# Where the operands of single-pass matmuls begin in SBUF: 128 and 448 past a multiple of 512 bytes, or at the multiple

## The chip, the cores and the metric

The kernel runs on one core of one Trainium2 chip. The metric is the device time of one execution in microseconds, the median over several runs; lower is better.

## What is computed

Two transformer blocks run one after the other on one sequence of 256 tokens and 1024 features, all in float32 with weights from HBM. The first block (two layers) has a SwiGLU on either side of a mixer; the mixer of layer 0 joins a spatial gate with a three-way sparse attention, that of layer 1 a causal pooling with a diagonal state-space scan. The second block (two layers) has a mixer of three branches (retention, a gated recurrence, a sliding-window attention with sinks), then a SwiGLU in layer 0 and a top-2 mixture of eight experts in layer 1. Cut to what matters here:

```python
def swiglu(h, w_gate, w_up, w_down):
    return (jax.nn.silu(h @ w_gate) * (h @ w_up)) @ w_down

# first block, each layer:
x = x + 0.5 * swiglu(rmsnorm(x, g0), ...)
x = x + mixer(rmsnorm(x, g1))
x = x + 0.5 * swiglu(rmsnorm(x, g2), ...)
# second block, each layer:
proj = h @ w_in[layer]                       # 1024 x 11776
merged = sig(ga) * y_a + sig(gb) * y_b + sig(gc) * y_c
h = layer_norm(ALPHA * h + merged @ w_o[layer])
h = layer_norm(ALPHA * h + (swiglu_2(h) if layer == 0 else moe_swiglu(h)))
```

Nearly all of the arithmetic is products of the 256 tokens with weight matrices that are each read once.

## The kernel before, in words

**Weights as a stream.** The host packs all weights in the order of their use into chunks of 128 partitions x 2048 float32 (1 MB): 332 "dense" chunks, then 336 for the experts. `Stream.load` (L142) brings a chunk into one of four `raw` buffers (eleven in the expert stage) on SP's queue. `Stream.split_to` cuts it into pieces of 1024 columns: ScalarE rounds a piece to the reduced type float32r (`wh`, L159), VectorE subtracts to get the rest (`wl`, L160). `Stream.get` hands out slices of 512 columns or less.

**Single-pass matmuls.** A float32 product is made of three matmuls of float32r operands, each of one pass, summed in PSUM: high x high, and twice high x low. `mm3w` (L252 on) holds the weights stationary and streams the activations: 128 stationary columns, 256 moving ones (`xh`, `xl`, and `hh`, `hl` within a SwiGLU). `mm3x` holds the activations stationary and streams 512 weight columns: some projections of the mixers (`proj_x_steps`), the last output projection, and all expert matmuls (`gate_up`, `down`: stationary `gxh`, `gxl`, `mhh`, `mhl`). All go through `mm` (L250). There are 18,709 such matmuls in the program. Small products that need full precision run in plain float32 and are not the matter here.

**Where tiles lie.** Every tile is a byte range that is the same in all partitions. Pools follow each other in SBUF from low to high addresses: `one` (residual `x`, `xh`, `xl`), `raw`, a small pool `two` of 320 bytes (a vector table and a constant column), `hi` and `lo` (four buffers each of `wh`, `wl`, 4096 bytes apart), `wk`, and then pools that open and close stage by stage. `gap(pool, n, name)` takes n unused bytes of a pool, so that what follows begins n bytes later. The large operand tiles have sizes that are multiples of 512 bytes, so where a slice begins modulo 512 is settled by where its tile begins. Modulo 512, before the change:

| stage | moving operand | stationary operand |
|---|---|---|
| SwiGLUs, mixers, weights stationary | xh, hh, ah, gh, ch, yh, oh: 128 | wh, wl: 448 |
| mixers, weights moving | wh, wl: 448 | xh, oh: 128 |
| experts, gate, up, down | wh, wl: 448 | gxh, mhh: 256 |
| experts, gather of tokens | P: 256 | xh: 128 |
| experts, return of rows | yhl: 128 | PT: 384 |

**Order.** The order of instructions on each engine is that of the recorded program; tiles wait for their last readers. The lines that matter are L186 to L198 (`Net.__init__`), L224 on (`setup`), the `gap` calls in `even`, `odd`, `moe`, `run`, `run_last`, and the argument `free` of `ffn_core`, which is a gap ahead of `hh`.

Of the kernel before, what the change touches and what calls it, by code (L numbers as in the profile page):

```python
# [9 lines left out]
F32 = mybir.dt.float32  # L10
# [25 lines left out]
N_RAW, N_EXTRA = 4, 7  # L36
# [72 lines left out]
VOFF, NVEC = {}, {}  # L109
# [8 lines left out]
class Stream:  # L118
# [3 lines left out]
    def __init__(self, tc, dram, pools, split_ahead=4, extra=None):  # L122

        self.tc, self.nc, self.dram = tc, tc.nc, dram
        self.raw_p, self.hi_p, self.lo_p = pools
        self.specs = []
        self.pos = 0
        self.raw, self.hi, self.lo = {}, {}, {}
        self.loaded = self.split = 0
        self.extra = extra  # L130
        self.ahead, self.split_ahead = N_RAW - 1 + (N_EXTRA if extra else 0), split_ahead
        self.total = dram.shape[0]
# [45 lines left out]
def gap(pool, n, name):  # L178

    pool.tile([128, n // 4], F32, name="gap_" + name)


class Net:
    def __init__(self, ctx, tc, a, consts):  # L186
        self.tc, self.nc, self.a = tc, tc.nc, a
        self.ctx = ctx
        self.cn = consts
        pool = lambda n, b, **k: ctx.enter_context(tc.tile_pool(name=n, bufs=b, **k))  # L190
        self.one = pool("one", 1)
        self.raw_p = pool("raw", N_RAW)
        self.two = pool("two", 1)
        self.hi_p, self.lo_p = pool("hi", 4), pool("lo", 4)
        self.wk = pool("wk", 2)
        self.pa = pool("pa", 4, space=PSUM)
        self.pb = pool("pb", 4, space=PSUM)
        self.ws = Stream(tc, a["dense"], (self.raw_p, self.hi_p, self.lo_p))  # L198
# [25 lines left out]
    def setup(self):  # L224
        nc = self.nc
        self.ctx1 = self.ctx.enter_context(ExitStack())
        one1 = self.ctx1.enter_context(self.tc.tile_pool(name="one1", bufs=1, reuse_waits="tile"))
        self.vecs = {v: p.tile([128, NVEC[v]], F32, name=v) for v, p in (("vecs1", one1), ("vecs2", self.two))}
        nc.scalar.dma_start(self.vecs["vecs1"], self.a["vecs1"])
        self.x = self.one.tile([128, KD, S], F32, name="x")  # L230
        self.ws.load_to(0, [lambda s=slice(2 * d, 2 * d + 2): nc.sync.dma_start(self.x[:, s], self.a["xt"][:, s])
                            for d in range(4)])
        self.ws.split_to(1)
        self.ws.load_to(1)
        self.ident = self.consts(self.one, "all")["ident"]
        nc.gpsimd.dma_start(self.vecs["vecs2"], self.a["vecs2"])
        self.ones = self.one.tile([128, 128], F32, name="ones")
        nc.vector.memset(self.ones, 1.0)
        self.mhalf = self.two.tile([128, 16], F32, name="mhalf")
        nc.vector.memset(self.mhalf, -0.5)  # L240
        self.xh = self.one.tile([128, KD, S], F32R, name="xh")
        self.xl = self.one.tile([128, KD, S], F32R, name="xl")
# [219 lines left out]
    def even(self):  # L462
# [5 lines left out]
        with tc.tile_pool(name="ev", bufs=1, reuse_waits="tile") as P:  # L468
# [8 lines left out]
            for i in range(2):  # L477
# [6 lines left out]
                v = kv.rearrange("p g (n r) -> p r g n", r=8)  # L484
# [44 lines left out]
                nc.scalar.activation(vt[:, t], o[t], AF.Copy, scale=rc[:, t:t + 1])  # L529


            gap(P, 96, "a")
            ah = P.tile([128, 4, S], F32R, name="ah")
            al = P.tile([128, 4, S], F32R, name="al")
            tr = nc.tensor.transpose
# [100 lines left out]
            rv = self.rstd_cols(ms[:, 1], 16, 1.0 / 64, 1e-5)  # L636
            nc.vector.tensor_mul(vg, vg, rv[:, :, None].to_broadcast([128, 16, 64]))
            gap(P, 320, "g")
            gh = P.tile([128, 4, S], F32R, name="gh")
            gl = P.tile([128, 4, S], F32R, name="gl")  # L640
# [142 lines left out]
    def odd(self):  # L783
# [1 line left out]
        factors = self.rms_in(self.vec("norm", 32, 8))  # L785
        w, idx = "od_w_in", (0,)
        with tc.tile_pool(name="od", bufs=1, reuse_waits="tile") as P:
            gap(P, 448, "od")
            pm = self.consts(P, "odd")["pool"]
            pw = self.load(P, "pw", [128, 4, 128], self.a["pw"])  # L790
            u = P.tile([128, 4, S], F32, name="s5u")
# [63 lines left out]
            def pooling():  # L855

                for o in self.proj_x_steps([(w, idx, 0, 512)], 512, self.xh, self.xl):
                    yield
                zc = P.tile([128, 2, 512], F32, name="zc")
                for t in range(2):  # L860
                    nc.scalar.activation(zc[:, t], o[t], AF.Copy, scale=rc[:, t:t + 1])
                for g in range(4):
                    b = self.pbank((128, 512), "a")
                    s = slice(128 * g, 128 * g + 128)
                    self.mm(b[:, :256], zc[:, 0, s], pm[:, 384 * g:384 * g + 256], True, False)
                    self.mm(b[:, 128:256], zc[:, 1, s], pm[:, 384 * g + 256:384 * g + 384], False, True)
                    pl = W.tile([128, S], F32, name="pl", tag="t256", bufs=4)
                    nc.scalar.activation(pl, b[:, :S], AF.Copy)
                    b = self.pbank((128, 512), "a")
                    self.mm(b[:, :S], pw[:, g], pl, True, True)  # L870
                    yc = W.tile([128, S], F32, name="yc", tag="t256", bufs=4)
                    nc.scalar.activation(yc, b[:, :S], AF.Copy, scale=self.vec("pscale", g))
                    self.split(ch[:, g], cl[:, g], yc)
                    if g % 2:
                        yield
                for d in range(KD // 2):
                    for n, b in enumerate(self.proj_t_steps([("od_w_out", idx, d * 256, 256)], ch, cl, 4)):
                        if n % 2:
                            yield
                    self.add_out(d, b)  # L880

            steps = pooling()
            bu, a, z, py = {}, {}, {}, {}
# [495 lines left out]
        self.ln_finish(self.vec("lnmix", 0, 8), self.vec("lnmix", 8, 8))  # L1379

    def ffn2(self):
        self.ffn_core("ffn_w_gate_2", "ffn_w_up_2", "ffn_w_down_2", (0,), (0,), None, self.residual2, free=128)
        self.ln_finish(self.vec("lnffn", 0, 8), self.vec("lnffn", 8, 8))

    def ln_stats(self, x):
# [35 lines left out]
    def moe(self):  # L1421
        nc, tc, W = self.nc, self.tc, self.wk
        V = nc.vector
        Z = self.mo
        x = self.hx
        C = self.consts(Z, "moe")
        gap(Z, 256, "mo")
        cr = Z.tile([128, 2, 128], F32R, name="cr")
        V.tensor_copy(cr[:, 0], C["before"])
        V.tensor_copy(cr[:, 1], self.ones)  # L1430
# [81 lines left out]
        def one_hot(ep):  # L1512
            P = Z.tile([128, 2, 2, 128], F32R, name="P")
            for e in range(2):
                for t in range(2):
                    V.tensor_scalar(P[:, t, e], C["iota"][:, :128], pos[:, t, 2 * ep + e:2 * ep + e + 1], None,
                                    op0=OP.is_equal)
            return P
# [72 lines left out]
        P = one_hot(0)  # L1591
        G = gather(P)
        for e in range(NE):
            y = None
            pend = None
            for fb in range(8):
# [9 lines left out]
                if fb == 3 and e % 2 and e + 1 < NE:  # L1606
                    P = one_hot(e // 2 + 1)
# [122 lines left out]
    def run(self):  # L1730
        tc = self.tc
        self.setup()
        with tc.tile_pool(name="evw", bufs=1, reuse_waits="tile") as P:
            steps = self.even_loads(P)
            self.ffn1(0, 0, steps, free=352)
            for _ in steps:
                pass
            self.even()
        with tc.tile_pool(name="s5p", bufs=1, reuse_waits="tile") as P2:
            with tc.tile_pool(name="s5q", bufs=1, reuse_waits="tile") as P:  # L1740
                steps = self.s5_params(P, P2)
                self.ffn1(0, 1, steps, free=128)
                self.ffn1(1, 0, steps, free=128)
                for _ in steps:
                    pass
            self.odd()
        self.ffn1(1, 1, after=self.between)
        self.ctx1.close()
        with tc.tile_pool(name="l2", bufs=1, reuse_waits="tile") as Q:
            self.l2 = Q  # L1750
            gap(Q, 128, "l2")
            self.layer0()
        self.ffn2()
        self.run_last()

    def run_last(self):

        tc = self.tc
        with ExitStack() as self.ctx2:
            self.mo = self.ctx2.enter_context(tc.tile_pool(name="hxp", bufs=1))  # L1760
            with tc.tile_pool(name="l2b", bufs=1, reuse_waits="tile") as Q:
                self.l2 = Q
                gap(Q, 128, "l2")
                self.layer1()
            self.mo = self.ctx2.enter_context(tc.tile_pool(name="mo", bufs=1, reuse_waits="tile"))
            self.moe()
            self.overflow()
            self.out()
# [86 lines left out]
```

## Time and profile before

| | us |
|---|---|
| median of 3 runs | 3130.25 |
| the three runs | 3129.6, 3130.25, 3144.65 |
| the profiled execution's own time | 3141.89 |
| its span in the trace | 3140.1 |

The profile comes from one execution that took 3141.89 us, 11.6 us more than the median; its 1.8 us beside the span lie ahead of the first and behind the last instruction. The columns of the page: PE is TensorE's matmuls, PEld its weight loads, which overlap the matmuls, DVE VectorE, ACT ScalarE, POOL GpSimd. A matmul's record begins where it begins to stream and ends when its last result is written, so records of successive matmuls overlap: the time that a matmul costs is the step from its start to the start of the next, not its own duration. A row of a timeline gives start, duration, engine, line and operands; a row of windows gives a stretch and, per engine, busy time and the count of records that touch the stretch.

### The profile page before, as it was taken

To read this page: it belongs to the slowest core of one execution; us is meant where nothing else is said; L and a number is where in the kernel's file an instruction comes from. 1 tells how busy PE (TensorE), PEld (TensorE's weight loads), DVE (VectorE), ACT (ScalarE), POOL (GpSimd) and SP (SyncE) were. 2 spreads that over 40 slices of the span, in tenths; PEclk is the share of its full clock that TensorE was granted. 3 is DMA by queue.
4 is the path that set the end of the run, shared out by engine and by line. 5 is a ranking of instruction groups with operands and counts; after the bars stand their busy time and mean duration, and the time that the engine had idled before them with its cause. 6 is when DMAs were issued, how large, how long until landed. Compare 5 with 4: busy or idle time off the path is not lost. (4 is left out here: it accounts for less than half of the span.)

```text
span 3140.1 us, 51830 instructions
## 1 busy us (share of the span) xinstructions
PE 3046.8 (97%) x20841; PEld 2748.4 (88%) x20841; DVE 2341.3 (75%) x3444; ACT 1855.7 (59%) x2527; POOL 187.2 (6%) x159
## 2 busy tenths in 40 slices
PE   8999999999999999999999999989999999999998
PEld 8997999996899899899998898977787878878876
DVE  6667777868766675566556765568999899999888
ACT  5456555542543655554546654447777777777775
POOL 1000000002102000112010000010000000000000
PEclk9999999999999999999999999989999999999999
DMA  7542555551454333454553334658998998998994
GB/s 251 209 163 95 178 190 185 184 204 54 175 188 177 127 130 135 174 191 154 195 188 121 121 124 178 250 191 336 347 367 330 348 359 338 360 353 332 358 359 152
DMA packets 97414, 696.37 MB, mean 222 GB/s; under 512 B 10880, under 2 KB 11232, under 8 KB 13456
## 3 DMA queue, kind: packets, MB, share of 16 engines
q1 hardware_dynamic: 95184, 685.81, 59.3%
q0 software_dynamic: 752, 3.85, 0.4%
q8 instruction: 165, 2.70, 0.3%
q10 hardware_dynamic: 1232, 3.34, 0.3%
q14 instruction: 81, 0.66, 0.1%
HBM read 691.92 MB, written 1.05 MB: 221 GB/s over the span
## 5 line engine op out<-in xcount | busy, mean ns | idle before, releaser
L160 DVE TENSOR_TENSOR wl<-raw,wh 128x1024 fp32r<-128x1024 f32 x1299 | 1587.0, 1238 | 499.9 <-ACT wh L159 492.0
L159 ACT ACTIVATE wh<-raw 128x1024 fp32r<-128x1024 f32 x1299 | 1363.1, 1060 | 800.2 <-PE pa L250 639.8
L250 PE MATMUL pa<-xh,wh 128*128 128x256 f32 x3072 | 867.5, 283 | 13.2 <-ACT wh L159 9.8
L250 PE MATMUL pa<-xl,wh 128*128 128x256 f32 x3072 | 865.4, 282 | 4.1 <-DVE xl L348 3.9
L250 PE MATMUL pa<-xh,wl 128*128 128x256 f32 x3072 | 864.2, 281 | 0.5 <-DVE wl L160 0.5
L250 PEld LDWEIGHTS pa<-xh,wh 128*128 128x128 f32 x3072 | 585.5, 191 | 17.3 <-ACT wh L159 9.8
L250 PEld LDWEIGHTS pa<-xl,wh 128*128 128x128 f32 x3072 | 584.2, 190 | 6.6 <-DVE xl L348 5.3
L250 PEld LDWEIGHTS pa<-xh,wl 128*128 128x128 f32 x3072 | 587.3, 191 | 1.1 <-DVE wl L160 0.8
L250 PE MATMUL pa<-wl,gxh 128*128 128x512 f32 x896 | 354.6, 396 | 1.3 <-DVE wl L160 1.3
L250 PE MATMUL pa<-wh,gxl 128*128 128x512 f32 x896 | 354.2, 395 | 0.0
L250 PE MATMUL pa<-wh,gxh 128*128 128x512 f32 x896 | 323.2, 395 | 0.0
L250 PE MATMUL pa<-hh,wl 128*128 128x256 f32 x880 | 246.0, 280 | 0.0
L250 PE MATMUL pa<-hl,wh 128*128 128x256 f32 x880 | 245.9, 279 | 0.0
L250 PE MATMUL pa<-hh,wh 128*128 128x256 f32 x880 | 245.8, 279 | 0.0
L250 PEld LDWEIGHTS pa<-wl,gxh 128*128 128x128 f32 x896 | 168.4, 188 | 43.9 <-DVE wl L160 3.4
L250 PEld LDWEIGHTS pa<-wh,gxh 128*128 128x128 f32 x896 | 168.4, 188 | 40.7
L250 PEld LDWEIGHTS pa<-wh,gxl 128*128 128x128 f32 x896 | 168.3, 188 | 40.5
L250 PE MATMUL pb<-wl,mhh 128*128 128x512 f32 x448 | 179.2, 400 | 0.0
L250 PE MATMUL pb<-wh,mhl 128*128 128x512 f32 x448 | 177.8, 397 | 0.0
L250 PEld LDWEIGHTS pa<-hh,wl 128*128 128x128 f32 x880 | 167.3, 190 | 0.1
L250 PEld LDWEIGHTS pa<-hh,wh 128*128 128x128 f32 x880 | 165.5, 188 | 0.0
L250 PEld LDWEIGHTS pa<-hl,wh 128*128 128x128 f32 x880 | 165.2, 188 | 0.0
(506 smaller groups left out, 4041.3 us busy)
## 6 DMA issues: line engine op xcount, KB each, us to landing
raw<-in_moe SPq DMA_DIRECT2D x336, 1024.0 KB, 5.5
raw<-in_dense SPq DMA_DIRECT2D x315, 1024.0 KB, 4.8
c_lay<-in_c_lay POOLq DMA_DIRECT2D x2, 1152.0 KB, 6.9
x<-in_xt SPq DMA_DIRECT2D x4, 256.0 KB, 5.8
raw<-in_dense SPq DMA_DIRECT2D x4, 256.0 KB, 6.7
w<-in_cw ACTq DMA_DIRECT2D x1, 1024.0 KB, 8.1
out_dram<-hx SPq DMA_DIRECT2D x2, 512.0 KB, 2.6
c_odd<-in_c_odd POOLq DMA_DIRECT2D x1, 768.0 KB, 4.5
```

The costliest lines, as they stand in the source:

```text
L159: self.nc.scalar.activation(h, src, AF.Copy)
L160: self.nc.vector.tensor_sub(l, src, h)
L250: self.nc.tensor.matmul(out, l, r, start=start, stop=stop, skip_group_check=True)
```

## The change

No operation, shape, buffer count or order changes. Pool `two` goes; its two tiles and 64 unused bytes stand at the front of `one`, which moves `x`, `xh`, `xl` and `raw`, `hi`, `lo` to multiples of 512. The gaps are set anew so that the operand tiles of each stage begin there too:

```diff
         self.one = pool("one", 1)
-        self.raw_p = pool("raw", N_RAW)
-        self.two = pool("two", 1)
-        self.hi_p, self.lo_p = pool("hi", 4), pool("lo", 4)
+        self.vecs = {"vecs2": self.one.tile([128, NVEC["vecs2"]], F32, name="vecs2")}
+        self.mhalf = self.one.tile([128, 16], F32, name="mhalf")
+        gap(self.one, 64, "x")
+        self.raw_p, self.hi_p, self.lo_p = pool("raw", N_RAW), pool("hi", 4), pool("lo", 4)
...
-            gap(P, 96, "a")
+            gap(P, 416, "a")
...
-            gap(P, 448, "od")
+            gap(P, 256, "od")
...
-        self.ffn_core("ffn_w_gate_2", "ffn_w_up_2", "ffn_w_down_2", (0,), (0,), None, self.residual2, free=128)
+        self.ffn_core("ffn_w_gate_2", "ffn_w_up_2", "ffn_w_down_2", (0,), (0,), None, self.residual2, free=448)
...
-        gap(Z, 256, "mo")
+        gap(Z, 448, "mo")
...
-            self.ffn1(0, 0, steps, free=352)
+            self.ffn1(0, 0, steps, free=160)
...
-                self.ffn1(0, 1, steps, free=128)
-                self.ffn1(1, 0, steps, free=128)
+                self.ffn1(0, 1, steps, free=448)
+                self.ffn1(1, 0, steps, free=448)
...
-        self.ffn1(1, 1, after=self.between)
+        self.ffn1(1, 1, after=self.between, free=320)
...
-            gap(Q, 128, "l2")
+            gap(Q, 448, "l2")
...
-                gap(Q, 128, "l2")
+                gap(Q, 64, "l2")
```

Behind it every moving and every stationary operand of the table above begins at 0 modulo 512, with three exceptions: in the second block's last mixer `oh`, `ol` begin at 128 (against 0 for the weights), `PT` begins at 128, and the tiny operand `selr` of the router at 448. The distance from the moving to the stationary operand modulo 512, which was 320 or 192, is 0 in nearly all matmuls. Tiles of other instructions shift along.

One wait moves on POOL's queue, since the tile that a load writes over has another neighbour now. Here is the place ahead of the second block's first mixer, where the constants of the mixer (`c_lay`) and a vector table are loaded. Before:

```order
63 L945 TENSOR_TENSOR acc<-acc 128x256 [waits Pool_49]
64 L207 DMA c_lay<-in_c_lay 128x2304 [waits DMAHW5_49,DMASW2_49,PE_49]
65 L207 DMA vecs_11692<-in_vecs 128x50 [waits DMASW3_49]
66 L1725 MEMSET KA_11694 128x512
67 L1725 MEMSET KB_11695 128x768
```

And in the change:

```order
63 L944 TENSOR_TENSOR acc<-acc 128x256 [waits Pool_49]
64 L207 DMA c_lay<-in_c_lay 128x2304 [waits DMASW3_49,DMAHW5_49,DMASW2_49,PE_49]
65 L207 DMA vecs_11691<-in_vecs 128x50
66 L1724 MEMSET KA_11693 128x512
67 L1724 MEMSET KB_11694 128x768
```

The first of the two loads waits for what the second had waited for: an earlier load on POOL's own queue.

## Rows read from the trace of the kernel before

**Rows 1.** Page, parts 1 and 5: shares and costliest groups.

```profile
PE 3046.8 (97%) x20841; PEld 2748.4 (88%) x20841; DVE 2341.3 (75%) x3444; ACT 1855.7 (59%) x2527; POOL 187.2 (6%) x159
...
L250 PE MATMUL pa<-xh,wh 128*128 128x256 f32 x3072 | 867.5, 283 | 13.2 <-ACT wh L159 9.8
...
L250 PE MATMUL pa<-wl,gxh 128*128 128x512 f32 x896 | 354.6, 396 | 1.3 <-DVE wl L160 1.3
...
L250 PE MATMUL pa<-hh,wl 128*128 128x256 f32 x880 | 246.0, 280 | 0.0
```

**Rows 2.** Timeline of PE, first SwiGLU: first and last of 51 matmuls.

```profile
99.80 0.28 PE L250 MATMUL pa<-xh,wl 128*128 128x256 f32 x1
...
105.47 0.28 PE L250 MATMUL pa<-xl,wh 128*128 128x256 f32 x1
```

**Rows 3.** Timeline of PE, second SwiGLU: first and last of 49 matmuls.

```profile
449.81 0.28 PE L250 MATMUL pa<-hh,wl 128*128 128x256 f32 x1
...
455.46 0.28 PE L250 MATMUL pa<-hh,wl 128*128 128x256 f32 x1
```

**Rows 4.** Windows, PE's L250: stretch, busy (x count), clock, DMA share, GB/s.

```profile
100.00:120.00 20.00, 20.00 (x179) 1.00 0.62 223
400.00:420.00 20.00, 20.00 (x172) 1.00 0.53 191
...
640.00:660.00 20.00, 20.00 (x172) 1.00 0.50 168
840.00:860.00 20.00, 20.00 (x172) 1.00 0.49 170
...
985.00:1005.00 20.00, 20.00 (x177) 1.00 0.60 211
1230.00:1250.00 20.00, 20.00 (x179) 1.00 0.55 199
1370.00:1390.00 20.00, 20.00 (x179) 1.00 0.58 211
...
1610.00:1630.00 20.00, 20.00 (x173) 1.00 0.54 191
1880.00:1900.00 20.00, 20.00 (x172) 1.00 0.46 167
2030.00:2050.00 20.00, 20.00 (x178) 1.00 0.53 192
```

**Rows 5.** Timeline of PE, experts, 512 columns: first and last of 21 matmuls.

```profile
2199.82 0.39 PE L250 MATMUL pa<-wh,gxh 128*128 128x512 f32 x1
...
2204.49 0.39 PE L250 MATMUL pa<-wh,gxl 128*128 128x512 f32 x1
```

**Rows 6.** Timeline of PE, last projection, 512 columns: ends of 22 matmuls.

```profile
2072.04 0.39 PE L250 MATMUL pa<-wh,ol 128*128 128x512 f32 x1
...
2076.84 0.40 PE L250 MATMUL pa<-wh,ol 128*128 128x512 f32 x1
```

**Rows 7.** Timeline of PE, 1026.5 to 1027 us: the two operands change places.

```profile
1026.66 0.28 PE L250 MATMUL pa<-xh,wl 128*128 128x256 f32 x1
1026.77 0.28 PE L250 MATMUL pa<-wh,xh 128*128 128x256 f32 x1
```

**Rows 8.** Timeline of PE, 2865.4 to 2866.4 us: gather of tokens, 256 columns.

```profile
2865.44 0.39 PE L250 MATMUL pb<-P,xh 128*128 128x256 f32 x2
...
2866.39 0.39 PE L250 MATMUL pb<-wl,mhh 128*128 128x512 f32 x1
```

**Rows 9.** Windows, experts: PE, PEld, DVE, ACT, POOL, clock, DMA, GB/s.

```profile
2160.00:2230.00 70.00, 70.00 (x312) 56.33 (x310) 64.14 (x63) 55.38 (x59) 0.00 (x0) 1.00 0.97 363
...
2930.00:2980.00 50.00, 50.00 (x223) 40.37 (x222) 44.97 (x41) 38.75 (x41) 0.00 (x0) 1.00 0.94 354
```

**Rows 10.** Tile c_lay: its load on POOL and its first reader.

```profile
L1061 DVE CUSTOM_DVE_ANT_0 ssm<-pb,c_lay x64: 280/356/422, 1038.7 to 1734.2; 128x128 f32<-128x128 f32 x32, 128x256 f32<-128x256 f32 x32
...
L207 POOL DMA_DIRECT2D c_lay<-in_c_lay x2: 578/590/601, 1004.3 to 1312.2; - x2
```

More of the change, by code (lines that the diff above doesn't have):

```diff
@@ L227, in setup @@
         one1 = self.ctx1.enter_context(self.tc.tile_pool(name="one1", bufs=1, reuse_waits="tile"))
-        self.vecs = {v: p.tile([128, NVEC[v]], F32, name=v) for v, p in (("vecs1", one1), ("vecs2", self.two))}
+        self.vecs["vecs1"] = one1.tile([128, NVEC["vecs1"]], F32, name="vecs1")
         nc.scalar.dma_start(self.vecs["vecs1"], self.a["vecs1"])
@@ L238, in setup @@
         nc.vector.memset(self.ones, 1.0)
-        self.mhalf = self.two.tile([128, 16], F32, name="mhalf")
         nc.vector.memset(self.mhalf, -0.5)
```

## Prediction

> **What bounds the kernel now.** I read the page first, then the timeline of PE stage by stage, then windows. The page says that TensorE is busy for 97% of the span and that its three dearest kinds of instruction are single-pass matmuls: 3,072 triples on `xh`, `xl`, 880 on `hh`, `hl`, and in the experts 896 on `gxh`, `gxl`, which wait for something for a few us in all [rows 1]. So nearly the whole span is a sum of matmuls, and what one costs is the step from its start to the next start. In the windows the granted clock is 1.00, the 2.4 GHz level, where a column per cycle would take 0.4167 ns: 106.7 ns for 256 columns and 213.3 ns for 512.
>
> The steps are longer than that, and not all the same:
> - In the first SwiGLU 50 steps take 105.47 - 99.80 = 5.67 us: 113.4 ns each [rows 2].
> - In the second 48 steps take 455.46 - 449.81 = 5.65 us: 117.7 ns each, though `wh`, `wl` lie at the same addresses, `hh` at the same offset modulo 512, and nothing waits [rows 3].
> - Windows of 20 us count 177 to 179 matmuls where the lower step holds, and 172 or 173 where the upper does (a record of 0.28 us that only touches the window counts too: 20.28 / 179 = 113.3 ns, 20.28 / 172 = 117.9 ns). Of these ten, spread over the stages with 256 columns, five show each [rows 4]. One step holds for hundreds of us and then gives way to the other.
> - In the experts 20 steps of 512 columns take 2204.49 - 2199.82 = 4.67 us: 233.5 ns [rows 5]. In the last output projection 21 take 2076.84 - 2072.04 = 4.80 us: 228.6 ns [rows 6]. The moving weights begin at 448 in both; the stationary operand begins at 256 in the first and at 128 in the second.
>
> So 6 to 10 per cent of a matmul's time are not columns, and this is the only thing that the change can touch at scale.
>
> **The change part by part.** It removes and adds no work on TensorE, VectorE, ScalarE or SP: the same rows in the same order, each at other addresses. I cost three things.
>
> First, the 256-column matmuls: 3 x 3,072 + 3 x 880 = 11,856 by the rows, and some 1,900 more by the code (the inner products of the mixers), 13,800 in all. Half of them take the upper step. The starts change from 128 (moving) and 448 (stationary) to 0 and 0. No row of the trace has 0 and 0 as a steady pair, so I bound it. What comes nearest in the distance of the two is a place where the operands change roles: while `xh` streams from 128, the next stationary load is `xh` too, from 128, a distance of 0. The step there, 1026.66 to 1026.77, is 0.11 us, as its neighbours at the lower step [rows 7]; a distance of 0 by itself costs nothing there. Nearest in the size of the multiple is the gather of tokens, where `P` streams from 256 against `xh` at 128, both multiples of 128: eight steps take 2866.39 - 2865.44 = 0.95 us, 118.8 ns [rows 8], though its PSUM banks are emptied in between, which may hold a part of that. So the bounds are all at 113.4 (13,800 / 2 x 4.3 ns = 30 us gained) and all at 118.8 (13,800 x (118.8 - 115.6) = 44 us lost). I take 0: the two steps come and go at one and the same placement, so what picks the step is not where the operands begin but how the two streams stand to each other in time when a stretch begins, and the change leaves that to the same chance.
>
> Second, the expert matmuls, 3 x 896 + 3 x 448 = 4,032 with 512 columns at 233.5 ns. They go from 448 against 256 to 0 against 0. Bounds: the step of the last output projection, (233.5 - 228.6) x 4,032 = 20 us gained, and as much again lost if the same difference goes the other way. I take 0, since the two stages differ in more than one thing (in the projection two matmuls in a row stream the same weights). DMA would let a gain through: it is at 0.94 to 0.97 of its share here [rows 9], and 2% less time would lift 0.95 to 0.97.
>
> Third, the wait on POOL: the load of `c_lay` also waits for an earlier load of its own queue. `c_lay` is issued at 1004.3 and first read by the scores at 1038.7 [rows 10]; 34 us lie between, behind it in the queue stand only the vector table and the memsets. It is covered; without that cover it would cost at most the difference of two loads, a few us. The work of ScalarE and VectorE on pieces moves by whole multiples of 64 bytes and I cost it at nothing: in the experts, where they are fullest, VectorE is busy for 64.14 of 70 us and TensorE for all 70 [rows 9], so a slower VectorE would show only past 9%.
>
> Sum: 0. The profiled execution took 3141.9 us and stays there; it stood 11.6 us over the median of 3130.25, which fits two steps whose shares differ from run to run. My forecast is the median, **3130 us**. A measurement of this kernel tells about 0.5% (16 us) from no change.
>
> A rule to weigh: the Trainium skill, "TensorE: Matmul & The Clock Gate", section "Step-by-step: what each phase is for", says that TensorE reads its moving operand and its next weights through two independent ports, so that a weight load takes nothing from the running matmul. By it no placement of one against the other could matter, and the sum would be 0, as mine. The trace gives it only half a yes: with the same moving start the step was 228.6 in one stage and 233.5 in another.
>
> **The rivals.**
> - *The lower step everywhere (faster).* If both steps come from requests of the two streams that meet, equal starts may keep them from meeting: 30 + 20 = 50 us gained, 3080. For it: a step that differs between [rows 5] and [rows 6] with only the stationary start and the reuse of weights to explain it. Against: the two steps at one placement [rows 2, 3].
> - *Both streams begin in the same place (slower).* Now the first read of the moving operand and that of the next weights fall on the same offset at the same moment, in every matmul; one has to stand back. Then all 256-column matmuls take the step of the gather, +44 us, and the experts lose another 4.9 ns each, +20: up to 64, about 3194; with the upper step alone, +30, 3160. It decides once a quarter more of the 256-column matmuls take the upper step (3,600 x 4.3 ns = 16 us). For it: [rows 8]. Against: [rows 7].
> - *The excess goes away whole (much faster).* If it comes from reads that straddle some boundary of 128 to 512 bytes, starts at the multiple remove it, down to a column per cycle: 13,800 x (115.6 - 106.7) = 123 us, and in the experts 4,032 x 20.2 = 81, of which DMA at 0.95 lets through about 5% of the some 950 us that these matmuls take, 47. That is 170 us, about 2960. Against: the tiles moved are read from end to end either way, and the moving tiles at 128 and at 448 show much the same excess per column. The Trainium skill, "TensorE: Matmul & The Clock Gate", section "Back-to-back issue gap", gives 262 and 518 cycles for 256 and 512 columns, 109.2 and 215.8 ns; worked out from that, as an estimate, the gain would end at some 160 us without the limit of DMA. The trace stands above that gap in every row here.
> - *The change does nothing, or undoes itself in part*: in the second block's last mixer the activations begin at 128 and the weights at 0, so whatever 0 and 0 does is left out there; that is part of my forecast's case.
>
> **How the numbers follow.** No effect of placement: 0.44, of which 0.33 end within 16 us, and 0.06 and 0.05 beyond it on either side, as the share of the upper step falls out (all of the 30 us is the most). The lower step everywhere: 0.26, of which 0.23 faster and 0.03 too little to tell. Streams that meet: 0.25, of which 0.22 slower and 0.03 too little to tell. The excess gone whole: 0.05. So faster 0.06 + 0.23 + 0.05 = 0.34, within 0.5% 0.33 + 0.03 + 0.03 = 0.39, slower 0.05 + 0.22 = 0.27. The likeliest case alone holds 3100 to 3160. The range has to reach into the cases on both sides: 3075, below the 50 us gained, to 3178, between the upper step alone and the whole of the second rival.
>
> **What would show it.** Right: both steps, 113 and 118 ns, still stand side by side in the SwiGLUs, and the experts stay at 233 ns. If the first rival holds, no window of 20 us counts under 177, and the expert step falls to 229. If the second does, the windows count 172 or fewer everywhere, and the last mixer, with its 128 against 0, differs from the other stages. If the third does, 20 us count about 190. A difference of ScalarE's or VectorE's mean per piece, or a span that grows in waits of TensorE and not in steps, would make the whole argument wrong.

## The result, and the profile after

The change made the kernel slower. Its four runs took 3169.32 to 3173.16 us, median **3171.53 us**; the kernel before, run beside it, took 3129.6 to 3144.65 us, median 3136.16. The ratio is 1.012, 95% interval 1.0095 to 1.0145. The forecast was 3130 us, no difference that can be told, with 0.39 on that and 0.27 on slower; the time lies inside the range of 3075 to 3178. Two executions below ran at a far lower mean granted clock and are left out of every comparison: one of six of the experts' half (5485.24 us at 0.77) and the only one of a fourth kernel with other distances (4617.95 us at 0.61).

The profiled execution took 3171.78 us (span 3170.0), 29.9 us more than that of before. Page of the kernel after, parts 1 and 5 (the helper that records the matmuls is L249 now), beside [rows 1]:

```profile
PE 3078.8 (97%) x20841; PEld 2803.7 (88%) x20841; DVE 2333.2 (74%) x3444; ACT 1852.4 (58%) x2527; POOL 186.5 (6%) x159
...
L160 DVE TENSOR_TENSOR wl<-raw,wh 128x1024 fp32r<-128x1024 f32 x1299 | 1579.0, 1233 | 531.4 <-ACT wh L159 494.4
L159 ACT ACTIVATE wh<-raw 128x1024 fp32r<-128x1024 f32 x1299 | 1359.9, 1058 | 835.9 <-PE pa L249 672.9
L249 PE MATMUL pa<-xh,wh 128*128 128x256 f32 x3072 | 879.0, 286 | 12.5 <-ACT wh L159 9.2
...
L249 PE MATMUL pa<-wl,gxh 128*128 128x512 f32 x896 | 349.4, 390 | 1.5 <-DVE wl L160 1.4
...
L249 PE MATMUL pa<-hh,wl 128*128 128x256 f32 x880 | 249.2, 283 | 0.0
```

TensorE is busy for 32.0 us more, in a span that is 29.9 us longer, so the time did not go into waits of it. VectorE and ScalarE take 1233 and 1058 ns for a piece (1238 and 1060 before), so they have no part in it. A 256-column matmul lasts 3 ns longer, a 512-column one of the experts 6 ns less: the two kinds went in opposite directions.

Windows of 20 us of TensorE's L249 in the kernel after (stretch, busy and count, clock, DMA share, GB/s), beside [rows 4]:

```profile
100.00:120.00 20.00, 20.00 (x169) 1.00 0.49 175
400.00:420.00 20.00, 20.00 (x170) 1.00 0.52 184
640.00:660.00 20.00, 20.00 (x169) 1.00 0.52 195
...
1370.00:1390.00 20.00, 20.00 (x169) 1.00 0.57 201
1610.00:1630.00 20.00, 20.00 (x169) 1.00 0.47 170
```

169 or 170 matmuls in each of the five, where before there were 172 to 179: one step of 20.28 / 169 = 120.0 ns has taken the place of the two, and it is longer than either. The timeline of the experts in the kernel after (start, duration, engine, line, operands), beside [rows 5], shows the other half:

```profile
2299.68 0.39 PE L249 MATMUL pa<-wl,gxh 128*128 128x512 f32 x1
...
2302.40 0.39 PE L249 MATMUL pa<-wl,gxh 128*128 128x512 f32 x1
```

Twelve steps take 2.72 us: 226.7 ns each, where before one took 233.5. In the last output projection, where weights at 0 stream against `oh` at 128, 27 steps from 2120.71 to 2126.98 take 6.27 us, 232.2 ns, where before one took 228.6 [rows 6]. In the mixer ahead of it, where `oh` and `ol` at 128 stream against weights at 0, the 329 steps of 256 columns have a mean of 118.7 ns and not 120.0.

The sum closes but for 6 us. Over the whole trace, the steps from one single-pass matmul to the next of the same width, at full clock and without a wait between, come to this: with 256 columns 13,467 steps of 115.42 ns before, now 119.86 ns, 13,467 x 4.44 = 59.8 us more; with 512 columns 4,436 steps of 232.87, now 227.47, 24.0 us less. Net that is 35.8 us lost, and the span grew by 29.9: all other steps together take some 6 us less, in several small parts.

### The profile page after: what moved, and what is told of

Its sections match the earlier page's. It is cut to its first block, busy times and chain, and to the rows that moved or that the text cites. A ratio compares the mean times of both kernels' runs of the same rounds, so it can differ in the third digit from the quotient of the medians.

```text
span 3170.0 us, 51831 instructions
## 1 busy us (share of the span) xinstructions
PE 3078.8 (97%) x20841; PEld 2803.7 (88%) x20841; DVE 2333.2 (74%) x3444; ACT 1852.4 (58%) x2527; POOL 186.5 (6%) x159
## 5 line engine op out<-in xcount | busy, mean ns | idle before, releaser
L160 DVE TENSOR_TENSOR wl<-raw,wh 128x1024 fp32r<-128x1024 f32 x1299 | 1579.0, 1233 | 531.4 <-ACT wh L159 494.4
L159 ACT ACTIVATE wh<-raw 128x1024 fp32r<-128x1024 f32 x1299 | 1359.9, 1058 | 835.9 <-PE pa L249 672.9
L249 PE MATMUL pa<-xh,wh 128*128 128x256 f32 x3072 | 879.0, 286 | 12.5 <-ACT wh L159 9.2
L249 PE MATMUL pa<-xl,wh 128*128 128x256 f32 x3072 | 877.0, 286 | 3.7 <-DVE xl L347 3.7
L249 PE MATMUL pa<-xh,wl 128*128 128x256 f32 x3072 | 876.2, 285 | 0.5 <-DVE wl L160 0.5
L249 PEld LDWEIGHTS pa<-xh,wh 128*128 128x128 f32 x3072 | 594.8, 194 | 16.7 <-ACT wh L159 9.2
L249 PEld LDWEIGHTS pa<-xl,wh 128*128 128x128 f32 x3072 | 594.5, 194 | 5.8 <-DVE xl L347 4.5
L249 PEld LDWEIGHTS pa<-xh,wl 128*128 128x128 f32 x3072 | 594.6, 194 | 1.1 <-DVE wl L160 0.8
L249 PE MATMUL pa<-wl,gxh 128*128 128x512 f32 x896 | 349.4, 390 | 1.5 <-DVE wl L160 1.4
L249 PE MATMUL pa<-wh,gxl 128*128 128x512 f32 x896 | 348.8, 389 | 0.0
L249 PE MATMUL pa<-wh,gxh 128*128 128x512 f32 x896 | 317.5, 389 | 0.0
L249 PE MATMUL pa<-hh,wl 128*128 128x256 f32 x880 | 249.2, 283 | 0.0
L249 PE MATMUL pa<-hl,wh 128*128 128x256 f32 x880 | 249.2, 283 | 0.0
L249 PE MATMUL pa<-hh,wh 128*128 128x256 f32 x880 | 249.0, 283 | 0.0
L249 PEld LDWEIGHTS pa<-wl,gxh 128*128 128x128 f32 x896 | 168.2, 188 | 38.9 <-DVE wl L160 4.1
L249 PEld LDWEIGHTS pa<-wh,gxh 128*128 128x128 f32 x896 | 168.2, 188 | 35.1
L249 PEld LDWEIGHTS pa<-wh,gxl 128*128 128x128 f32 x896 | 168.2, 188 | 34.7
L249 PE MATMUL pb<-wl,mhh 128*128 128x512 f32 x448 | 177.1, 395 | 0.0
L249 PE MATMUL pb<-wh,mhl 128*128 128x512 f32 x448 | 175.6, 392 | 0.0
L249 PEld LDWEIGHTS pa<-hh,wl 128*128 128x128 f32 x880 | 168.9, 192 | 0.1
L249 PEld LDWEIGHTS pa<-hl,wh 128*128 128x128 f32 x880 | 168.9, 192 | 0.0
L249 PEld LDWEIGHTS pa<-hh,wh 128*128 128x128 f32 x880 | 168.9, 192 | 0.0
```

What stands on the lines that cost most here:

```text
L159: self.nc.scalar.activation(h, src, AF.Copy)
L160: self.nc.vector.tensor_sub(l, src, h)
L249: self.nc.tensor.matmul(out, l, r, start=start, stop=stop, skip_group_check=True)
```

## The experiments

In all of them "distance" is the start of the stationary operand minus that of the moving one, modulo 512 bytes. The theory formed on the two traces: the distance sets the step. 256 columns take 120 ns at 0, and 113 or 118 at 320; 512 columns take 226.7 at 0, 229 at 192, 233.3 at 320. The rival is the change's own wording: that operands begin at multiples of 512.

### Distance 0 without any multiple of 512

```diff
-        self.two = pool("two", 1)
         self.hi_p, self.lo_p = pool("hi", 4), pool("lo", 4)
+        self.two = pool("two", 1)
...
-        gap(Z, 256, "mo")
+        gap(Z, 128, "mo")
```

> The kernel before, with pool two moved behind lo, so that weights begin at 128 as the activations do, and the gap of the experts 128, so that their stationary operands begin at 128 too: the distance from moving to stationary operand is 0 in all large matmuls, but none begins at a multiple of 512. Theory of the distance: steps as in the changed kernel, 120 ns with 256 columns everywhere and 227 ns in the experts, 3165 to 3178 us. Theory of the multiple (what counts is that starts are multiples of 512): the two steps of before, 113 and 118, come back, experts at 229 to 233, 3115 to 3145 us.

Measured: 3170.73 us (3169.6 to 3171.72) against 3147.64 before in the same runs, ratio 1.0075 (1.0047 to 1.0102); in microseconds the same as the change's 3171.53. Windows of L250 in this kernel:

```profile
100.00:120.00 20.00, 20.00 (x169) 1.00 0.48 178
...
1610.00:1630.00 20.00, 20.00 (x169) 1.00 0.45 169
```

The timeline of its experts, first and last of 13 matmuls:

```profile
2299.82 0.39 PE L250 MATMUL pa<-wh,gxh 128*128 128x512 f32 x1
...
2302.54 0.39 PE L250 MATMUL pa<-wh,gxh 128*128 128x512 f32 x1
```

Twelve steps take 2.72 us; the mean of all is 226.9 ns. So the multiples of 512 have nothing to do with it; both steps of the change come with distance 0 and starts at 128.

### The experts' half alone

```diff
-        gap(Z, 256, "mo")
+        gap(Z, 448, "mo")
```

> The kernel before with one number changed: the gap of the experts 448 for 256, so that their stationary operands begin at 448 as the moving weights do. Theory of the distance: the expert step falls from 233.3 to 227 ns in 4,032 matmuls, 25 to 27 us off, ratio to before 0.991; the 256-column steps stay as before. Theory of the multiple: the experts stay at 233 ns, ratio 1.00.

Measured: 3126.82 us (five executions, 3123.48 to 3128.91) against 3147.64, ratio 0.9937 (0.9914 to 0.996): faster than both kernels. Timeline of its experts:

```profile
2300.00 0.39 PE L250 MATMUL pa<-wh,gxh 128*128 128x512 f32 x1
...
2302.72 0.39 PE L250 MATMUL pb<-wh,mhh 128*128 128x512 f32 x1
```

Twelve steps take 2.72 us, and the mean of all is 226.9 ns, while the windows of 256 columns still hold 172 to 179. Up to the experts this is the program of before at the same addresses, yet its steps fall out otherwise (100 to 120 us, 400 to 420 and 1370 to 1390, beside [rows 4]):

```profile
100.00:120.00 20.00, 20.00 (x179) 1.00 0.59 214
400.00:420.00 20.00, 20.00 (x179) 1.00 0.64 212
...
1370.00:1390.00 20.00, 20.00 (x172) 1.00 0.48 185
```

So which of the two steps a stretch takes at distance 320 differed between two executions of one placement. The spread of the kernel before fits this: 3123 to 3159 us over all its runs here, where the three kernels with 256 columns at distance 0 stay within 4 us each in their four runs. It is not shown to be the whole of it: this kernel, with both steps, spreads by 5 us in its five.

### The 256-column half alone

As the first experiment, but with `gap(Z, 448, "mo")`: the experts stay at distance 320.

> Of the change's two halves only the one of the 256-column matmuls: they stand at distance 0 (weights at 128, as the activations), while the experts keep their distance of 320 (stationary operands at 448). Theory: the 256-column step is 120.0 ns everywhere as after the change, the experts stay at 233 ns; with 13,489 steps at 119.9 in place of about 115.4 that is some 60 us more than before, 3185 to 3200 us, ratio 1.016 to 1.022, and 20 us count 169 matmuls in the SwiGLUs. Together with the experts alone (19.7 us less, ratio 0.9937) the halves then add up to what the whole change did. Rival (the halves are not independent, or part of the loss came from elsewhere in the change): a ratio under 1.012.

Measured: 3192.88 us (3191.83 to 3193.82) against 3143.7, ratio 1.0159 (1.0139 to 1.0178). The time is the one expected; the ratio is at the lower end, since before had a median of 3143.7 us beside it, where it had 3131.9 beside the last experiment below.

```profile
640.00:660.00 20.00, 20.00 (x169) 1.00 0.50 184
900.00:920.00 20.00, 20.00 (x169) 1.00 0.53 181
```

And its experts:

```profile
2299.68 0.40 PE L250 MATMUL pa<-wl,gxh 128*128 128x512 f32 x1
...
2302.48 0.40 PE L250 MATMUL pa<-wl,gxh 128*128 128x512 f32 x1
```

The step is 120 ns; that of the experts is 2.80 us / 12 = 233.3. The halves add up within the spread of before: from here to distance 0 in the experts too it is 3192.88 - 3170.73 = 22.2 us, and from before to the experts' half 3147.64 - 3126.82 = 20.8.

### Other distances, in the network

Each SwiGLU has its own gap ahead of `hh`, so one kernel tries five distances. Three kernels did, with edits such as

```diff
-            self.ffn1(0, 0, steps, free=352)
+            self.ffn1(0, 0, steps, free=96)
...
-                self.ffn1(0, 1, steps, free=128)
+                self.ffn1(0, 1, steps, free=320)
```

> As scan a, with hh at 64, 0, 416, 352, 160 (distance 384, 448, 32, 96, 288; the last three are no multiples of 64) and the expert operands at 128 (distance 192). Theory of the distance: no down projection at 120 ns; the expert step differs from 233. If what counts is a start at a multiple of 64, the last three SwiGLUs' down projections are slower than the first two by a few ns. Theory of the multiple: hh at 0 against weights at 448 makes no 120, since the weights are not at 0; all at 113 or 118.

> Distances (start of the stationary weights minus start of the moving operand, modulo 512) in the five SwiGLUs: 64, 128, 192, 256, 352 for hh, in the order of the program; xh stays at 320; the experts go to 64. Theory (the distance alone sets the step, and 0 is the worst place for 256 columns): each of the five hh stretches shows one step of its own between 113 and 119.5 ns, none reaches 120.0, and 20 us count 170 to 179 matmuls; the experts at 64 stand between 226.8 and 229.6 ns, since 0 gave 226.8 and 192 gave 229.6. Rival (320 alone is special, all others are alike): all five hh stretches at 118 to 118.5 ns. Rival (the chance of the execution decides, not the distance): the two steps 113.3 and 117.8 mix in the hh stretches too.

> Distances of hh in the five SwiGLUs: 160, 224, 416, 480, 448; xh stays at 320; the experts go to 128. Theory: again one step for each distance, between 113 and 119.5 ns, 117.7 at 448 as it was before at that distance; the experts at 128 between 229 and 233 ns. Rival (320 alone is special): all five at 118 to 118.5 ns. Rival (chance): both steps mix in all of them.

Measured: 3135.16, 3150.44 and 3149.37 us, one run each. Windows of L250 within the first three SwiGLUs' `hh`, second scan (distances 64, 128, 192):

```profile
150.00:170.00 20.00, 20.00 (x179) 1.00 0.54 199
455.00:475.00 20.00, 20.00 (x169) 1.00 0.49 184
640.00:660.00 20.00, 20.00 (x173) 1.00 0.50 178
```

And third scan (160, 224, 416):

```profile
150.00:170.00 20.00, 20.00 (x169) 1.00 0.47 174
455.00:475.00 20.00, 20.00 (x174) 1.00 0.54 191
640.00:660.00 20.00, 20.00 (x170) 1.00 0.54 187
```

Mean steps of `hh`, 528 matmuls each, in ns: 113.3 at 64; 120.0 at 128, 160, 256 and 416; 119.2 at 96; 117.8 at 192 and 448; 118.3 to 118.7 at 32, 288, 352 and 384; 116.7 at 224 and 480. So 320 alone is not special (64 is as low), and 0 is not alone in being bad: 128 and 256 took 120.0, which the theory had ruled out for the second scan. At 96 and 352 the mean hides a change within the stretch: the first quarter ran at 117.3, the last two at 120.0 and 118.7.

Among `hh` only 64 reached 113.3, and `xh`, which stayed at 320, did so too. But 192 can as well. In a projection of the second block's mixers the weights stream from 448 against `xh` at 128, a distance of 192; in the third scan the timeline there begins and ends so:

```profile
1665.19 0.28 PE L250 MATMUL pa<-wh,xl 128*128 128x256 f32 x1
...
1669.27 0.28 PE L250 MATMUL pa<-wh,xl 128*128 128x256 f32 x1
```

Thirty-six steps take 4.08 us, 113.3 ns; at the same place the two other scans took 117.8. The experts went to 229.5 ns at 192 as expected, but to 233.3 at 64, where 226.8 to 229.6 had been expected, and to 232.8 at 128.

### Weights split: high ones at distance 0, low ones at 320

```diff
+        self.hi_p = pool("hi", 4)
         self.two = pool("two", 1)
-        self.hi_p, self.lo_p = pool("hi", 4), pool("lo", 4)
+        self.lo_p = pool("lo", 4)
```

> wh begins at 128 modulo 512, as xh and hh do (distance 0), wl at 448 (distance 320). The three matmuls of a product run as wh against xh, wh against xl, wl against xh. Theory A (what counts is the moving operand of a matmul against the weights that are loaded beside it, those of the next matmul): the step of wh-xh, beside which wh is loaded again, is 120, that of wh-xl, beside which wl is loaded, 113 or 118, that of wl-xh, beside which the next wh is loaded, 120; a triple 353 to 358 ns. Theory B (a matmul's own two operands): wh-xh and wh-xl 120, wl-xh 113 or 118. Theory C (a common state of the stretch, not the single pair): all three steps equal, or mixed without order. By A and B alike the whole kernel lands between 3140 and 3165 us.

Measured: 3161.72 us, one run. Timeline of TensorE in the second SwiGLU:

```profile
459.78 0.28 PE L251 MATMUL pa<-hh,wl 128*128 128x256 f32 x1
459.90 0.28 PE L251 MATMUL pa<-hh,wh 128*128 128x256 f32 x1
460.01 0.28 PE L251 MATMUL pa<-hl,wh 128*128 128x256 f32 x1
...
469.67 0.28 PE L251 MATMUL pa<-hh,wl 128*128 128x256 f32 x1
```

Eighty-four steps take 9.89 us, 117.7 ns, and the three of a triple are 0.12, 0.11 and 0.12: means of 118.3 for `wl` and 117.3 to 117.7 for `wh`. Neither the 120 of distance 0 nor the 113.3 of 320 appears. Theories A and B fall, each of which gave the matmuls of a triple different steps; the step belongs to the whole sequence (theory C).

### The matmuls by themselves

The network is left out. Two moving and two stationary tiles; stretches of 60 matmuls in the kernel's order:

```python
for k in range(triples):
    m = [T[x][:, om + (k % 4) * 512:om + (k % 4) * 512 + n] for x in ("ma", "mb")]
    s = [T[x][:, os + (k % 8) * 128:os + (k % 8) * 128 + 128] for x in ("sa", "sb")]
    for i, (a, c) in enumerate(((0, 0), (0, 1), (1, 0))):
        nc.tensor.matmul(out, s[a], m[c], start=k == 0 and i == 0, stop=k == triples - 1 and i == 2, ...)
```

> Leaves the network out: 128 x 256 activations are rounded into two moving and two stationary tiles, then stretches of 60 single-pass matmuls run in the kernel's order of high and low operands, moving tiles at 128 modulo 512, stationary ones at each of the 16 distances in steps of 32 bytes, 256 and 512 columns in turn; all of it three times with no other engine at work, then eight stretches of 256 columns at distance 0 and 64 with the moving tile at four other places, then the 16 distances once more while ScalarE and VectorE copy pieces of 1024 columns without a pause. Theory (the distance modulo 256 of the two streams that TensorE itself reads sets the step): with the other engines idle 256 columns take 120 ns at 0, 128, 160 and 256, about 117.8 at 192 and 448, 116.7 at 224 and 480, 113.3 or 117.8 at 64 and 320; 512 columns 226.7 at 0, 229.5 at 192, 232 to 233.3 at 64, 128 and 320; and the last part repeats this. Rival A (the other engines' reads and writes of SBUF make the difference): with the others idle all distances give one step, and the differences come with the traffic of the last part. Rival B (the place of an operand counts, not the distance): the eight stretches differ with the moving tile's place. Rival C (the two steps at one distance come from how a stretch starts): distances 64 and 320 give different steps in the three rounds, the others the same one each time.

ScalarE's copies, which depend on little, ran beside the first round and not in the last part, as windows of this kernel show (PE, PEld, DVE, ACT, POOL, clock, DMA share): ScalarE alone beside the first round, nothing beside the second and third, VectorE alone in the last part.

```profile
40.00:340.00 300.00, 300.00 (x1718) 262.52 (x1717) 0.00 (x0) 280.70 (x265) 0.00 (x0) 1.00 0.00 1
400.00:1000.00 600.00, 600.00 (x3408) 523.72 (x3407) 0.00 (x0) 0.00 (x0) 0.00 (x0) 1.00 0.00 1
1110.00:1400.00 290.00, 290.00 (x1645) 253.12 (x1645) 282.09 (x231) 0.00 (x0) 0.00 (x0) 1.00 0.00 1
```

The steps do not mind: at every distance the four passes agree within 0.2 ns once a stretch runs. Timeline of the first and last matmul of four stretches of the first round, 256 and 512 columns at distance 0, 512 at 320, 256 at 64:

```profile
35.44 0.28 PE L22 MATMUL bank<-ma,sa 128*128 128x256 f32 x1
...
42.51 0.28 PE L22 MATMUL bank<-ma,sb 128*128 128x256 f32 x1
42.63 0.40 PE L22 MATMUL bank<-ma,sa 128*128 128x512 f32 x1
...
56.03 0.39 PE L22 MATMUL bank<-ma,sb 128*128 128x512 f32 x1
...
63.33 0.39 PE L22 MATMUL bank<-ma,sa 128*128 128x512 f32 x1
...
77.09 0.39 PE L22 MATMUL bank<-ma,sb 128*128 128x512 f32 x1
...
119.19 0.28 PE L22 MATMUL bank<-ma,sa 128*128 128x256 f32 x1
...
126.14 0.28 PE L22 MATMUL bank<-ma,sb 128*128 128x256 f32 x1
```

Fifty-nine steps each: 7.07 us is 120 ns, 13.40 is 227.1, 13.76 is 233.2, 6.95 is 117.8. All distances, second half of each stretch, in ns:

| distance | 256 columns | 512 columns | distance + 256 | 256 columns | 512 columns |
|---|---|---|---|---|---|
| 0 | 120.0 | 226.7 | 256 | 120.0 | 226.7 |
| 32 | 118.4 | 233.4 | 288 | 118.3 | 233.4 |
| 64 | 117.8 | 233.4 | 320 | 117.8 | 233.4 |
| 96 | 118.7 | 234.3 | 352 | 117.4 | 234.2 |
| 128 | 118.8 | 232.7 | 384 | 119.9 | 233.5 |
| 160 | 120.0 | 233.4 | 416 | 120.0 | 233.4 |
| 192 | 117.8 | 229.0 | 448 | 117.8 | 229.0 |
| 224 | 116.6 | 233.3 | 480 | 117.9 | 233.2 |

Rival A falls: no other engine is needed, nor any load from HBM. Rival B falls at distance 0: with the moving tile at 0, 192, 256 and 384 the step is 120.0 each time. The columns repeat after 256 bytes, with 512 columns within 0.8 ns, with 256 within 1.3; the next experiment shows where that 1.3 comes from. At 128 and 480 the steps are not those of the network (118.8 and 117.9, where 120 and 116.7 had been expected). At distance 64, three of the four places of the moving tile gave 117.8 and one, the first after a stretch at distance 0, gave 113.3; Rival C's point, that the start of a stretch decides there, was left open by this, since the three rounds gave 117.8 each.

### What picks one of the two steps

```python
stretch(nc, bank, T, 512, 0, 320, 10)    # the same lead each time
event()                                  # one of 39, all of them twice
stretch(nc, bank, T, 256, 0, 64, 20)     # read here
```

> Leaves the network out, as the matmuls alone did. 78 times: 30 matmuls of 512 columns at distance 320, then one event, then 60 matmuls of 256 columns at distance 64, whose step is read. The events, all of them twice: 60 matmuls of 256 columns at each of the 16 distances; 3, 6, 12 or 24 at distance 0; one matmul of another width (32 to 448 columns); a wait for ScalarE of eight lengths. Theory (the step at this distance is a state that the stretch enters at its start and keeps): both rounds agree event by event, the step is 113.3 or 117.8 through a whole stretch and nothing between; stretches at distance 0 lead to 113.3, stretches at 64 or 320 to 117.8. Rival (chance): the two rounds differ in several events, at the same program. Rival (a matter of the slot that the event leaves off by): one matmul of another width is enough to change the state, and waits do so as well.

Timeline of three of the stretches that are read, first and last matmul: behind 60 matmuls at distance 0, behind 60 at distance 64, and behind a wait for ScalarE.

```profile
49.14 0.28 PE L22 MATMUL bank<-ma,sa 128*128 128x256 f32 x1
...
56.09 0.28 PE L22 MATMUL bank<-ma,sb 128*128 128x256 f32 x1
...
90.91 0.28 PE L22 MATMUL bank<-ma,sa 128*128 128x256 f32 x1
...
97.59 0.28 PE L22 MATMUL bank<-ma,sb 128*128 128x256 f32 x1
...
593.86 0.39 PE L22 MATMUL bank<-ma,sa 128*128 128x256 f32 x1 [0.92 <-ACT bank L74]
...
600.66 0.28 PE L22 MATMUL bank<-ma,sb 128*128 128x256 f32 x1
```

6.95 us is 117.8 ns a step, 6.68 is 113.2; the third has longer steps at its start and 113.3 ns from the fourth matmul on. Of the 78 stretches each ends at 113.3 or at 117.8, none between, and holds it from its fourth matmul on, a few behind another width from a little later; the two rounds agree in all 39 events. A wait for ScalarE led to 113.3 all 16 times. So did stretches at 12 of the 16 distances. Those at 0, 192, 256 and 448 led to 117.8, the reverse of what was expected of 0, 64 and 320. Of shorter stretches at distance 0, 3 and 6 matmuls led to 113.3, 12 and 24 to 117.8. In the last experiment a stretch behind distance 0 did take 113.3, with the moving tile in another place, so the distance of what came before is not all that counts. A single matmul of another width was enough to decide: 64, 192, 224, 288 and 384 columns led to 113.3, the six other widths to 117.8. The rival of chance falls here: the state is set by what came just before, and kept. In the network, where loads and the other engines shift what comes before, it differs between executions; that last link is argued, not shown.

The stretches ahead of those show a second thing. Here all 16 distances have the same 30 matmuls ahead of them, and with that each distance and the one 256 bytes on agree within 0.1 ns: 117.4 at 96 and 352, 118.8 at 128 and 384, 116.7 at 224 and 480. The first and last of 60 matmuls at 96:

```profile
104.70 0.28 PE L22 MATMUL bank<-ma,sa 128*128 128x256 f32 x1
...
111.62 0.28 PE L22 MATMUL bank<-ma,sb 128*128 128x256 f32 x1
```

That is 6.92 us or 117.3 ns a step, where the table has 118.7. So the period of 256 bytes is exact with the same start, and more distances than 64 and 320 have a second step: 118.7 and 120.0 beside 117.4 at 96, 120.0 beside 118.8 at 128, 117.9 beside 116.7 at 224, each there or 256 bytes on, in one of the kernels. At 0 and 160 no steady step but 120.0 was seen.

### Distance 64 for 256 columns, 0 in the experts

```diff
-        self.two = pool("two", 1)
+        gap(pool("pad", 1), 64, "pad")
         self.hi_p, self.lo_p = pool("hi", 4), pool("lo", 4)
+        self.two = pool("two", 1)
...
-        gap(Z, 256, "mo")
+        gap(Z, 128, "mo")
```

(and 64 bytes less in the other gaps).

> The weights begin at 192 modulo 512 and the activations at 128, so the 256-column matmuls stand at distance 64 in place of 320; the experts' stationary operands begin at 192, distance 0. Theory (period of 256, both steps by chance): the 256-column matmuls show 113.3 and 117.8 ns in turn, as at 320, the experts 226.8 to 228; 3100 to 3135 us, ratio to before 0.985 to 1.0. Rival (distance 64 holds the lower step alone, as its 528 matmuls did in the first SwiGLU of the scan): 113.3 ns in all stages, 20 us count 177 to 179 throughout, 3090 to 3105 us.

Measured: 3118.56 us (3109.66 to 3121.54) against 3131.87, ratio 0.9945 (0.9924 to 0.9965). Windows of L251, first and third SwiGLU:

```profile
100.00:120.00 20.00, 20.00 (x172) 1.00 0.51 179
...
640.00:660.00 20.00, 20.00 (x179) 1.00 0.60 211
```

Both steps again, so the rival that 64 holds the lower step alone falls. This kernel and the experts' half are the two that were shown to beat both the kernel before and the change; by their intervals they can't be told apart. So moving the 256-column matmuls from distance 320 to 64 brought nothing that can be told, as a period of 256 bytes would have it.

## Why the prediction was wrong

**What bounds the kernel** was right: the time is a sum of matmul steps, and the difference of 29.9 us between the profiled executions is one of steps, 59.8 lost and 24.0 gained, but for some 6 us.

**First term, 256 columns, taken as 0 between 30 gained and 44 lost: the step that failed.** It measured 59.8 us lost, outside its bounds. Two readings of the prediction led to the 0. "What picks the step is not where the operands begin" took two steps at one placement as proof that placement doesn't matter. The runs show both at once: the distance sets which steps there are (one, of 120.0 ns, at 0; two, 113.3 and 117.8, at 320), and what came before picks among them. And [rows 7], one step of 0.11 us at distance 0, was read as "a distance of 0 by itself costs nothing there". That was one hand-over amid triples at another distance, and a single pair does not show its own distance's step: in the kernel with split weights pairs at distance 0 took 117.3 to 117.7 ns, beside others at 320, not 120. The upper bound came from [rows 8], whose distance was 384 and not 0.

**Second term, the experts, taken as 0 within 20 either way.** It measured 24.0 us gained. The sign of the lower bound was right and its size nearly so, by luck: [rows 6] was a step at distance 192, and 0 has one of its own, 226.7, which puts the gain 4 us beyond that bound. The reuse of weights in the projection, my reason to distrust that row, wasn't the cause: the experts at 192 took 229.5, as the projection did at 228.6 to 228.9.

**Third term, POOL's wait, 0: right.** The load of `c_lay` was issued at 1030.9 us and first read at 1067.3, 36.4 us later, where it had been 34 [rows 10]. ScalarE and VectorE, costed at nothing: right.

**The rivals.** Streams that begin in the same place had the right sign for 256 columns and for the whole, and both of its signs came: 172 matmuls or fewer in every window, and another step in the last mixer. It took the step from the gather, 118.8, where it is 120.0, and gave the experts a loss. Its mechanism isn't shown: distance 160, where the starts differ, takes the same 120.0, and for 512 columns equal starts are the best. The lower step everywhere had the experts' gain, 20 us, and was wrong on 256 columns. I put the two as one choice for both widths; the answer is one for each width, and the sum of +59.8 and -24.0 lies beside both. The excess did not go away anywhere: no steady step came below 113.3 or 226.7 ns, and the 109.2 and 215.8 ns that the rival worked out from the Trainium skill, "TensorE: Matmul & The Clock Gate", "Back-to-back issue gap", were not reached.

The rule that was weighed, of two independent ports (the Trainium skill, "TensorE: Matmul & The Clock Gate", "Step-by-step: what each phase is for"), does not hold here as the prediction took it, that no placement of one operand against the other could matter: with nothing but matmuls and their loads at work, moving a stationary tile by 64 bytes changes the step from 120.0 to 117.8 or 113.3 ns, or with 512 columns from 226.7 to 233.4. What the matmul waits for in the longer steps, no run shows.

## What to carry to other kernels

Where a kernel is bound by back-to-back float32r matmuls, each with a new stationary operand, the start of the stationary operand against the moving one, modulo 256 bytes, is worth up to 6% of a step with 256 moving columns and 3% with 512, and the best distance depends on that number. Here 0 was best for 512 columns and among the worst for 256; for 256 columns 64 or 320 was as good as any. What could be gained was the experts' distance alone (ratio 0.9937), since the kernel before stood at 320 already. Try it by shifting one tile, read it from counts of matmuls per window, and set it apart for each stage. Two values at one placement do not clear placement of blame: ask which values there are at another.

## What the runs showed of the hardware that was not expected

- A stretch of 256-column matmuls at distance 64, 192 or 320 has two steady steps, 113.3 and 117.8 ns, 4% apart, and 96, 128 and 224 have two or three of their own, 1.2 to 1.3 ns apart. In the matmuls alone it keeps the one it starts with for its 60 matmuls; in the network, in the trace of before, for up to 179 us without a break. A wait of TensorE led to the lower one 16 times in 16 in the matmuls alone, at distance 64.
- Widths answer in opposite ways: distance 0 is among the worst for 256 columns (120.0 ns) and the best for 512 (226.7).
- All steady steps at full clock stand above a column per cycle, 106.7 and 213.3 ns, at every one of the 16 distances. That the excess comes from reads of the two streams that meet in the same part of SBUF would fit the repeat after 256 bytes; no run here shows the meeting itself, nor why equal starts are bad for one width and best for the other.
